# When low parts are stated, what small operations count for, and which jobs wait for which, in the front stage of a hybrid decoder layer

## The chip, the cores and the metric

The kernel runs on one core of a Trainium2 chip. The metric is the device time of one launch in microseconds (us). Engines: PE (TensorE, matmuls; PEld its weight loads), DVE (VectorE), ACT (ScalarE), POOL (GpSimd) and SP (SyncE, which issues the weight transfers).

## The reference, cut to what matters

One decoder layer for 256 tokens of width 2048, in float32:

```python
h = rms_norm(x, ln1)
proj = h @ w_in       # GDN q|k|v, beta, decay, z; MoBA q|k|v; gate A, gate B
y_a = gated_deltanet(qkv, beta, decay, z, ...) @ w_branch_a   # 8 heads, conv, delta rule
y_b = moba_attention(rope(q), rope(k), v) @ w_branch_b        # 8 heads, causal softmax
x = x + (sigmoid(gate_a) * y_a + sigmoid(gate_b) * y_b) @ w_out
h = rms_norm(x, ln2)
u = causal_dwconv(h @ w_up)
x = x + (silu(u_gate) * u_val) @ w_down
return rms_norm(x, final_norm)
```

## The kernel before

Each product of a weight block with the activations is made of three products in fp32r: the weight's high part with both parts of the activations, and its low part with the high part of the activations. A weight half tile of 128x1024 arrives by SP into `wraw`; ACT casts it to the high part `wh`, and DVE subtracts that from the raw weight, which gives the low part `wl` (`split`, L191; `load_half`, L214). There are four buffers each for `wh` and `wl`; the cast of a later half tile needs a buffer that PE has finished with.

The program is a front stage (all products with `w_in`), then the branch products, the output product, up and down. The front stage makes, for four groups of two heads, the projections for the gated delta rule (three `gdn` chunks of a convolution, one `z`), the MoBA projections (two `moba` chunks and `v` for two groups at a time), then sixteen gate chunks. Between these main matmuls it works off the small work of the heads: convolutions, the triangular solve and the delta rule (`gdn`, L633), the attention (`moba`, L867), decay and rotary.

In this stage nothing is reordered: on PE, DVE, ACT and POOL the order is that in which the program states the instructions (`manual_schedule`, L965). What sets it is an account. Each small job is a generator. `main_mm` (L177) states a main matmul, and after every 1700 units of the account, which are 16 matmuls of 128x256, it calls `tick` (L139). A tick lowers the account `load` of DVE, ACT and POOL by 1700 ns, and lets each job that is due go on to its next `yield`, if DVE's and ACT's account is under `ROOM` (quick jobs, the convolutions, have 1000 more). What a job states is added to the account by `Metered` (L84): the elements per partition times a rate plus a fixed sum per instruction. A job that yields "land" comes back `LAND` ns after its transfer.

Weight halves are stated where PE's count of main matmuls asks for them (`pump`, L156; `take`, L169): the ACT cast and, right behind it, the DVE subtraction. DVE works strictly through its own queue, so a subtraction whose cast is not over holds everything behind it.

Names used later. In `gdn`: `gam` decay factors, `jk` squared norms, `ssq` their transposes in psum, `X` and `tm` the pairs of small operations of the triangular solve (`Xa` its matrix, brought by POOL), `vb` the values that are updated step by step, `w1` (L825) the product that takes `vb`, `pot` the last transposes. In `moba`: `sc` the score products, `s_` the softmax tile with its row maxima (`largest`) and its final scaling (`share`, L911), `pT` the transposes of `s_` on PE (L932 to 934). `un`, `kq`, `vt` belong to the convolutions, `R1` is the reciprocal norm of the tokens. Psum has eight banks: three for main products, five that rotate among the small products, so that a small product in a bank waits for whoever reads the bank's former contents. Lists such as `early`, `seen`, `ended`, `clear` are gates: the job of a later group yields until the job of the former group has put itself on the list.

Of the kernel before, what the change touches and what calls it, by code (L numbers as in the profile page):

```python
# [11 lines left out]
F32 = mybir.dt.float32  # L12
# [7 lines left out]
P = 128  # L20
# [8 lines left out]
EVERY = 1700  # L29
ROOM = 2300  # L30
TABLE = 1220
ISSUE = 560
MORE = 11
LAND = 5200
TABLES = (AF.Exp, AF.Sigmoid, AF.Silu, AF.Sqrt, AF.Sin)
# [43 lines left out]
def layer_kernel(ctx: ExitStack, tc: tile.TileContext, w_first, xT, pos, cst, vec, convw, ffw, bdv,  # L79
# [4 lines left out]
    class Metered:  # L84


        def __init__(self, eng, name, per, each):
            self.eng, self.name, self.per, self.each, self.table = eng, name, per, each, None

        def __getattr__(self, op):  # L90
            f = getattr(self.eng, op)

            def run(*args, **kw):
                n = max([a.free_size() for a in (*args, *kw.values()) if hasattr(a, "free_size")], default=0)
                if op == "reciprocal":
                    n *= 6
                if op == "dma_start":
                    n = ISSUE
                func = [a for a in (*args, *kw.values()) if isinstance(a, type(AF.Exp)) and a in TABLES]
                extra = TABLE if func and func[0] != self.table else 0  # L100
                self.table = func[0] if func else self.table
                met(self.name, n * self.per + self.each, extra)
                return f(*args, **kw)  # L103

            return run

    pool = Metered(nc.gpsimd, "pool", 1.0, 0)
    act, dve = Metered(nc.scalar, "act", 0.87, 110), Metered(nc.vector, "dve", 1.03, 60)

# [14 lines left out]
    def met(name, n, more=0.0):  # L124
        load[name] += n + more
# [13 lines left out]
    def tick():  # L139
        clock[0] += EVERY  # L140
        for e in load:
            load[e] = max(load[e] - EVERY, 0.0)
        for jobs, most, soon_ in ((quick, ROOM + 1000, EVERY), (bg, ROOM, 0)):
            for it in list(jobs):
                if max(load["dve"], load["act"]) < most and ready.get(id(it), 0.0) <= clock[0] + soon_:
                    step(jobs, it)

    def flushed(jobs):
        while jobs:
            step(jobs, jobs[0])  # L150
# [18 lines left out]
    def take():  # L169
        n = taken[0]  # L170
        taken[0] += 1
        due[0] = 2 * n + 4
        passed[0] = 0
        pump()
        return n, made[2 * n:2 * n + 2]

# [14 lines left out]
    def split(hi, lo, src):  # L191
        highs.append(act.copy(hi, src))
        return low(hi, lo, src)
# [3 lines left out]

    lows, highs, again = [], [], []

# [14 lines left out]
    def load_half(raw, h, piece=HALF, at=0, into=None):  # L214
        wh, wl = halves(at, into)
        for o in range(0, HALF, piece):
            lows.append(split(wh[:, o:o + piece], wl[:, o:o + piece], raw[:, h * HALF + o:h * HALF + o + piece]))
        return wh, wl
# [355 lines left out]

    left, early, ended, joined, turned, seen, clear = [], [], [], [], [], [], []
    order_st = ExitStack()
# [46 lines left out]
    def dram(t, offset, *ap):  # L623
        return bass.AP(tensor=t.tensor, offset=t.offset + offset, ap=[list(x) for x in ap])
# [8 lines left out]
    def gdn(h0, kq, v):  # L633
# [31 lines left out]
        if left:  # L665
            turned_out()
            left.clear()
        dve.tensor_tensor(gam[:, :, 0::2, :], gam[:, :, 0:2, :], nm[:, None, None, :].to_broadcast([P, 2, 2, P]), op=ALU.add)

# [13 lines left out]
        for j in range(2):  # L683
            c = 8 + h0 + j
            for q, a in enumerate((0, 2, 1)):
                act.activation(gam[:, j, q, :], gam[:, j, q, :], AF.Exp, bias=cols[:, a, c:c + 1])
        yield
        aq0 = gl.tile([P, 2, 2, T], F32, name="aq0")
        aq1 = gl.tile([P, 2, 2, P], F32, name="aq1")
# [25 lines left out]
        pool.dma_start(dA[2:4, :P].rearrange("j s c -> s j c"), aq1[:, :, 0, :])  # L715
        while 2 * len(early) < h0:
            yield
        X = gl.tile([P, 160], F32, name="X", bufs=1)
        pool.tensor_copy(X, C["rows"])
        yield "land"  # L720
        dC = dr.tile([16, 32, 32], F32, name="dC")
        for e in range(2):
            pool.dma_start(dC[8 * e:8 * e + 8], dram(dA, e * 32 * (P + 1), (64 * (P + 1), 8), (P, 32), (1, 32)))
        yield "land"
        Xa = gl.tile([P, 33 * 32], F32, name="Xa", bufs=1)
        pool.dma_start(Xa[:, :1024], dram(dC, 0, (1024, 16), (0, 8), (1, 1024)))
        yield "land"
        pool.memset(r3(Xa, 33)[:, :, 0:1], -1.0)
# [14 lines left out]
        yield  # L743
        while 2 * len(seen) < h0:
            yield
        for q in range(4):
            pool.dma_start(S1[32 * q:32 * q + 32, :, 32 * q:32 * q + 32],
                           dram(dA, q * 64 * (P + 1) + 32, (P, 32), (2 * (P + 1) * P, 2), (1, 32)))

# [20 lines left out]
        while 2 * len(ended) < h0:  # L770
            yield
        pool.dma_start(E.rearrange("p e i c -> p (e i) c"), dram(dE, 0, (32, P), (4096, 4), (1, 32)))
        for j in range(2):
            pool.dma_start(S2[64 * j:64 * j + 64, :, 64 * j:64 * j + 64],
                           dram(dA, j * (P + 1) * P + 64, (P, 64), (2 * (P + 1) * P, 2), (1, 64)))
# [12 lines left out]
        yield  # L788
        seen.append(h0)
        Y = gl.tile([P, 2, 4, 32], F32, name="Y", bufs=1)  # L790
# [20 lines left out]
        for i in range(2):  # L811
# [10 lines left out]
            dve.tensor_tensor(vb[:, i, 1], vb[:, i, 1], pz, op=ALU.subtract)  # L822
            yield
            p1_ = sdt("w1")[:, :P]
# [4 lines left out]
            if i == 0:  # L829
                pr = r3(sdt("r1"), P)  # L830
                for j in range(2):
                    pe.matmul(pr[:, j, :], aq0[:, j, 0, P:], u[:, j, :], start=True, stop=True)
                yield
                for j in range(2):
                    for b in range(2):
                        o = slice(64 * j, 64 * j + 64)
                        dve.tensor_tensor(vb[o, 1, b], vb[o, 1, b], pr[64 * b:64 * b + 64, j, :], op=ALU.subtract)
                yield

# [16 lines left out]
        for p in range(4):  # L856
            act.mul(ot[:, p], po[:, p], st[:, 7, p:p + 1])
        yield
        pot = r3(sdt("pot"), T)
# [4 lines left out]
        yv = ya[:, h0:h0 + 2, :]  # L864
        dve.scalar_tensor_tensor(yv, pot, gnv, yv, op0=ALU.mult, op1=ALU.mult)

    def moba(h0, q, k, v):  # L867
# [58 lines left out]
        share(1)  # L926
        yield
        pps = []
# [29 lines left out]
    def delta(gr):  # L958
# [5 lines left out]
        if gr == 0:  # L964
            order_st.enter_context(tc.manual_schedule(engines={  # L965
                mybir.EngineType.DVE, mybir.EngineType.Activation, mybir.EngineType.Pool,
                mybir.EngineType.PE}))
            load.update(dve=2400.0, act=0.0, pool=0.0)
            bg.append(decay())

# [37 lines left out]
    def values_of():  # L1008
# [13 lines left out]
        v4 = m.tile([P, 2, 2 * T], F32, name="v_")  # L1022
        for i in range(2):
            act.mul(v4[:, i, :], ps[i], cols[:, 5 + i, 0:1])
        return v4
# [39 lines left out]
    for c in range(2 + MORE, 16):  # L1065
        gate(c, gts[c])
    flushed(quick)
    order_st.close()
    yp = y_st.enter_context(tc.tile_pool(name="yp", bufs=1, side="right", reuse_waits="tile"))
# [221 lines left out]
```

## Time and profile before

| what | value |
|---|---|
| median of 3 runs | 1463.87 us (1463.02 to 1464.78) |
| the profiled execution | 1462.9 us, of which the span 1461.1 us |
| mean granted TensorE clock of it | 0.996 |
| PE busy | 1439.3 us, 99% of the span |
| DVE busy | 964.5 us, 66% |
| ACT busy | 766.2 us, 52% |
| POOL busy | 186.0 us, 13% |

The span is the time from the first to the last instruction that the profiler saw. In the rows of the profile, L103 stands for every operation of ACT, DVE and POOL, because `Metered` makes them all from one line; there the names of the tiles tell which is which. A bracket at the end of a timeline row gives the idle time ahead of the instruction and what ended it.

### The profile page before, as it was taken

What the parts mean: (1) busy time and instruction counts of PE and PEld (TensorE: products, weight loads), DVE (VectorE), ACT (ScalarE), POOL (GpSimd) and SP (SyncE); (2) the same over time, 40 slices, a digit from 0 to 9 for tenths busy, and PEclk for the clock granted to TensorE, in tenths of its full rate; (3) what the DMA queues carried; (4) which work ended last, traced back from release to release, by engine and by line L of the source; (5) the groups of instructions that cost most, each with busy time, mean ns of one, the idle gap of its engine ahead of it and who ended that gap; (6) DMA issues with size and microseconds to landing.
All of it is one profiled execution on the core that took longest, in us unless ns stands there. A gap on an engine that the chain in (4) does not pass through costs nothing.

```text
span 1461.1 us, 26969 instructions
## 1 busy us (share of the span) xinstructions
PE 1439.3 (99%) x11271; PEld 1380.7 (94%) x11271; DVE 964.5 (66%) x1385; ACT 766.2 (52%) x1091; POOL 186.0 (13%) x237
## 2 busy tenths in 40 slices
PE   9999899999999999999999999999999999999998
PEld 9989898989899999999999999999999998888886
DVE  7778877786754556767776666666666666654454
ACT  7655555655564644445455545455455554444444
POOL 0003130314120300100121111111111110000000
PEclk9999999999999999999999999999999999999999
DMA  8456464646445555556685555555555555555552
GB/s 312 174 191 228 161 202 163 203 161 207 158 165 172 176 195 196 194 211 216 217 270 194 201 194 185 198 202 182 194 203 190 188 200 180 199 197 202 186 192 112
DMA packets 46347, 283.81 MB, mean 194 GB/s; under 512 B 7505, under 2 KB 8689, under 8 KB 14353
## 3 DMA queue, kind: packets, MB, share of 16 engines
q1 hardware_dynamic: 39200, 270.36, 53.4%
q0 software_dynamic: 6304, 9.63, 2.6%
q8 instruction: 88, 1.44, 0.4%
q10 hardware_dynamic: 720, 2.10, 0.4%
q14 instruction: 35, 0.28, 0.1%
HBM read 275.34 MB, written 3.82 MB: 191 GB/s over the span
## 4 chain that ended last, share of the span: by engine, by line
PE 92%; DVE 5%; ACT 2%; issue 1%; POOL 0%; DVEq 0%; ACTq 0%; POOLq 0%
PE ps_up L178 33%; PE pd L120 16%; PE ps_gate L178 11%; PE ps_gdn L178 6%; PE ps_br L178 6%; PE ps_wo L178 6%; PE ps_moba L178 5%; PE ps_v L178 3%; DVE wl L103 2%; PE ps_gdn L351 2%; PE ps_z L178 1%; ACT wh L103 1%; PE g L120 1%; DVE tm L103 0%; DVE X L103 0%
## 5 line engine op out<-in xcount | busy, mean ns | idle before, releaser
L103 DVE TENSOR_TENSOR wl<-wraw,wh 128x1024 fp32r<-128x1024 f32 (+1 forms) x496 | 611.7, 1236 | 398.4 <-ACT wh L103 395.0
L103 ACT CAST wh<-wraw 128x1024 fp32r<-128x1024 f32 (+1 forms) x496 | 515.2, 1042 | 606.0 <-PE ps_up L178 194.2
L178 PE MATMUL ps_up<-h,wh 128*128 128x256 f32 x2816 | 479.2, 276 | 0.0
L178 PEld LDWEIGHTS ps_up<-h,wh 128*128 128x128 f32 x2816 | 423.8, 188 | 0.0
L178 PE MATMUL ps_up<-h,wl 128*128 128x256 f32 x1408 | 388.8, 276 | 0.0
L178 PEld LDWEIGHTS ps_up<-h,wl 128*128 128x128 f32 x1408 | 264.3, 188 | 0.0
L178 PE MATMUL ps_gate<-hc,wh 128*128 128x256 f32 x1024 | 180.6, 280 | 0.0
L178 PEld LDWEIGHTS ps_gate<-hc,wh 128*128 128x128 f32 x1024 | 156.4, 189 | 0.0
L178 PE MATMUL ps_gate<-hc,wl 128*128 128x256 f32 x512 | 143.1, 280 | 0.0
L120 PE MATMUL pd<-wl,ah 128*128 128x512 f32 x336 | 125.4, 389 | 0.0
L120 PE MATMUL pd<-wh,al 128*128 128x512 f32 x336 | 124.4, 389 | 0.0
L120 PE MATMUL pd<-wh,ah 128*128 128x512 f32 x336 | 115.5, 389 | 0.0
L103 POOL TENSOR_TENSOR acts<-sg,cvf 128x256 f32<-128x256 f32 x44 | 62.8, 1428 | 408.1 <-ACT sg L103 396.8
L178 PE MATMUL ps_gdn<-hc,wh 128*128 128x256 f32 x640 | 111.9, 279 | 0.0
L178 PEld LDWEIGHTS ps_gdn<-hc,wh 128*128 128x128 f32 x640 | 97.2, 188 | 0.5 <-issue 0.4
L178 PEld LDWEIGHTS ps_gate<-hc,wl 128*128 128x128 f32 x512 | 97.0, 190 | 0.0
L178 PE MATMUL ps_moba<-hc,wh 128*128 128x256 f32 x512 | 90.3, 279 | 0.0
L178 PE MATMUL ps_gdn<-hc,wl 128*128 128x256 f32 x320 | 89.2, 279 | 0.5 <-DVE wl L103 0.5
L178 PE MATMUL ps_wo<-mc,wh 128*128 128x256 f32 x512 | 87.1, 276 | 0.0
L178 PEld LDWEIGHTS ps_moba<-hc,wh 128*128 128x128 f32 x512 | 78.0, 188 | 0.3 <-issue 0.2
L178 PEld LDWEIGHTS ps_wo<-mc,wh 128*128 128x128 f32 x512 | 77.0, 188 | 0.0
L120 PEld LDWEIGHTS pd<-wh,al 128*128 128x128 f32 x336 | 63.1, 188 | 13.1
(409 smaller groups left out, 1977.2 us busy)
## 6 DMA issues: line engine op xcount, KB each, us to landing
wraw<-in_w_up SPq DMA_DIRECT2D x88, 1024.0 KB, 4.9
wraw<-in_w_dn SPq DMA_DIRECT2D x44, 1024.0 KB, 4.9
wraw<-in_w_gate SPq DMA_DIRECT2D x32, 1024.0 KB, 4.9
wraw<-in_w_gdn SPq DMA_DIRECT2D x28, 1024.0 KB, 5.2
wraw<-in_w_moba SPq DMA_DIRECT2D x16, 1024.0 KB, 4.8
wraw<-in_w_o SPq DMA_DIRECT2D x16, 1024.0 KB, 4.9
wraw<-in_w_mv SPq DMA_DIRECT2D x8, 1024.0 KB, 4.9
wraw<-in_w_ba SPq DMA_DIRECT2D x8, 1024.0 KB, 4.9
```

The lines of the kernel that those rows point to most:

```text
L103: return f(*args, **kw)
L120: pe.matmul(ps, a, b, start=(start and i == 0), stop=(stop and i == n - 1), **kw)
L178: mark[0] = pe.matmul(ps, a, b, start=start, stop=stop, skip_group_check=True).ins
L351: pe.matmul(ps_two[b // 2][:, b % 2], wv[t][:, k - a, b * P:(b + 1) * P], hc.one(k, x_), start=(k == t == x_ == b % 2 == 0), stop=(k == KD ...
```

## The change

Four things are edited, all for the front stage.

1. In the front stage the DVE subtraction is no longer stated with its cast. It goes on a list `behind`, with the time at which ACT is through with the cast by the account. A tick states those whose time has come, ahead of the jobs; `take` states what is left of older tiles, in any case, before PE uses them.
2. DVE operations count at least 200 ns in the account. `ROOM` goes from 2300 to 3300, `LAND` from 5200 to 4700, `MORE` (gate chunks ahead of the end of the jobs) from 11 to 12.
3. Some gates move: `early` is waited for before `Xa` is fetched and not before `dC`; `seen` goes, and the transfers into `S1` go beside those into `S2`; a new gate `whole` stands ahead of `aq0`. The scaling of `v_` becomes a quick job, which waits for the column factors (`known`).
4. Two yields between `share` and the `pT` transposes in place of one, two ahead of `pot`.

```diff
-ROOM = 2300
+ROOM = 3300
-MORE = 11
-LAND = 5200
+MORE = 12
+WAIT = 2
+W1 = 1
+LAND = 4700
...
-                met(self.name, n * self.per + self.each, extra)
+                met(self.name, max(n * self.per + self.each, self.least), extra)
...
-    act, dve = Metered(nc.scalar, "act", 0.87, 110), Metered(nc.vector, "dve", 1.03, 60)
+    act, dve = Metered(nc.scalar, "act", 0.87, 110), Metered(nc.vector, "dve", 1.03, 60, 200)
...
             load[e] = max(load[e] - EVERY, 0.0)
+        while behind and behind[0][0] <= clock[0]:
+            behind.pop(0)[1]()
...
         pump()
+        while len(behind) > max(len(made) - 2 * n - 2, 0):
+            behind.pop(0)[1]()
...
-            lows.append(split(wh[:, o:o + piece], wl[:, o:o + piece], raw[:, h * HALF + o:h * HALF + o + piece]))
+            hi, lo, src = wh[:, o:o + piece], wl[:, o:o + piece], raw[:, h * HALF + o:h * HALF + o + piece]
+            if not stated:
+                lows.append(split(hi, lo, src))
+                continue
+            highs.append(act.copy(hi, src))
+            behind.append((clock[0] + load["act"], lambda hi=hi, lo=lo, src=src: lows.append(low(hi, lo, src))))
...
+        while 2 * len(whole) < h0 - 2:
+            yield
         aq0 = gl.tile([P, 2, 2, T], F32, name="aq0")
...
-        while 2 * len(early) < h0:
-            yield
-        X = gl.tile([P, 160], F32, name="X", bufs=1)
-        pool.tensor_copy(X, C["rows"])
         yield "land"
         dC = dr.tile([16, 32, 32], F32, name="dC")
...
+        while 2 * len(early) < h0:
+            yield
         Xa = gl.tile([P, 33 * 32], F32, name="Xa", bufs=1)
         pool.dma_start(Xa[:, :1024], dram(dC, 0, (1024, 16), (0, 8), (1, 1024)))
+        X = gl.tile([P, 160], F32, name="X", bufs=1)
+        pool.tensor_copy(X, C["rows"])
...
-        while 2 * len(seen) < h0:
-            yield
-        for q in range(4):
-            pool.dma_start(S1[32 * q:32 * q + 32, :, 32 * q:32 * q + 32],
-                           dram(dA, q * 64 * (P + 1) + 32, (P, 32), (2 * (P + 1) * P, 2), (1, 32)))
...
             dve.tensor_tensor(vb[:, i, 1], vb[:, i, 1], pz, op=ALU.subtract)
-            yield
+            yield from wait(W1)
...
         for p in range(4):
             act.mul(ot[:, p], po[:, p], st[:, 7, p:p + 1])
-        yield
+        yield from wait(2)
         pot = r3(sdt("pot"), T)
...
         share(1)
-        yield
+        yield from wait(WAIT)
         pps = []
...
             load.update(dve=2400.0, act=0.0, pool=0.0)
+            stated.append(True)
...
-        for i in range(2):
-            act.mul(v4[:, i, :], ps[i], cols[:, 5 + i, 0:1])
+
+        def scale():
+            while not known:
+                yield
+            for i in range(2):
+                act.mul(v4[:, i, :], ps[i], cols[:, 5 + i, 0:1])
+
+        quick.append(scale())
...
     flushed(quick)
+    while behind:
+        behind.pop(0)[1]()
+    stated.clear()
```

Three places show how the order on the engines moves. Numbers behind a name are those of the tile in that program, and differ between the two programs.

The first place is the start of the front stage on DVE. `R1` is the reciprocal norm of the tokens, `un` the first normed tile of a convolution, each `wl` a low part in the order in which PE uses them. Before:

```order
L103 TENSOR_TENSOR wl_455<-wraw_452,wh_454 128x1024
L103 TENSOR_TENSOR wl_459<-wraw_452,wh_458 128x1024
L103 RECIPROCAL R1_415<-R1_415 128x256
L103 TENSOR_TENSOR wl_465<-wraw_462,wh_464 128x1024
L103 TENSOR_TENSOR wl_469<-wraw_462,wh_468 128x1024
L103 TENSOR_TENSOR wl_500<-wraw_497,wh_499 128x1024
L103 TENSOR_TENSOR un_526<-ps_gdn_109,R1_415 128x512
```

After:

```order
L105 TENSOR_TENSOR wl_455<-wraw_452,wh_454 128x1024
L105 TENSOR_TENSOR sq1_0_111<-sq1_0_111,sq1_3_114 128x1024
L105 TENSOR_TENSOR wl_458<-wraw_452,wh_457 128x1024
L105 TENSOR_TENSOR sq1_0_111<-sq1_0_111 128x512
L105 TENSOR_TENSOR sq1_0_111<-sq1_0_111 128x256
L105 RECIPROCAL R1_415<-R1_415 128x256
L105 TENSOR_TENSOR un_486<-ps_gdn_109,R1_415 128x512
L105 TENSOR_TENSOR wl_463<-wraw_460,wh_462 128x1024
```

The sums of squares `sq1` now stand among the low parts, and `un` stands ahead of the third low part and no longer behind the fifth. On PE the matmul of `R1` moves from ahead of the first use of `wl_455` to 38 main matmuls later, among the uses of `wl_458`.

The same place on ACT, from the third cast on. Before:

```order
L103 CAST wh_464<-wraw_462 128x1024
L103 CAST wh_468<-wraw_462 128x1024
L103 ACT_TABLE_LOAD
L103 ACTIVATE R1_415<-R1_413,epst_65 128x256
L103 COPY z0_418<-ps_bd_396 16x256
L103 CAST wh_499<-wraw_497 128x1024
```

After:

```order
L105 CAST wh_462<-wraw_460 128x1024
L105 CAST wh_465<-wraw_460 128x1024
L105 CAST wh_499<-wraw_497 128x1024
L105 ACT_TABLE_LOAD
L105 ACTIVATE R1_415<-R1_413,epst_65 128x256
L105 COPY z0_418<-ps_bd_396 16x256
```

The cast of the fifth half tile moves from behind to ahead of the table load and `R1`.

The second place is on PE where the second group's `gdn` job begins its norms. `ssq_1981` is a transpose, `sc_1973` and `sc_1976` the score products of the first group's attention; in the program before the transposes `pT` stand in the neighbourhood and the score products far ahead. Before:

```order
L178 MATMUL ps_moba_2021<-hc_76,wl_1949 128x256
L178 MATMUL ps_moba_2021<-hc_76,wh_1948 128x256 x2
L178 MATMUL ps_moba_2021<-hc_76,wl_1949 128x256
L664 MATMUL ssq_2118<-ct_388,sqq_1946 128x128
L178 MATMUL ps_moba_2021<-hc_76,wh_1983 128x256 x2
```

After:

```order
L184 MATMUL ps_moba_1801<-hc_76,wl_1803 128x256
L903 MATMUL sc_1973<-qk1_997,qk0_871 128x256
L904 MATMUL sc_1973<-qk1_997,qk0_871 128x128
L903 MATMUL sc_1976<-qk1_997,qk0_871 128x256
L904 MATMUL sc_1976<-qk1_997,qk0_871 128x128
L675 MATMUL ssq_1981<-ct_388,sqq_1833 128x128
L184 MATMUL ps_moba_1988<-hc_76,wh_1846 128x256 x2
```

The transpose now follows the score products directly. It takes the psum bank of `sc_1973`, whose reader on DVE is `s__2018`; that is stated one tick later, behind `gam`, `jk`, `qk0`, a low part and three pairs `tm` and `X`.

The third place is on DVE, the final scaling of the second group's softmax tiles. Before, the tile is `s__2557`:

```order
L103 TENSOR_SCALAR s__2528<-s__2528,mx_2529 128x128
L103 TENSOR_TENSOR wl_2724<-wraw_2721,wh_2723 128x1024
L103 TENSOR_TENSOR tm_2738<-X_2304,Xa_2587 128x4x2
L103 TENSOR_REDUCE X_2304<-tm_2738 128x2x2
L103 TENSOR_TENSOR tm_2741<-X_2304,Xa_2587 128x4x3
L103 TENSOR_REDUCE X_2304<-tm_2741 128x2x2
L103 RECIPROCAL mx_2558<-mx_2558 128x2
L103 TENSOR_SCALAR s__2557<-s__2557,mx_2558 128x256
L103 TENSOR_SCALAR s__2557<-s__2557,mx_2558 128x128
```

After, the tile is `s__2599`:

```order
L105 TENSOR_TENSOR ya_425<-ps_z_2654,R1_415 128x512
L105 RECIPROCAL mx_2600<-mx_2600 128x2
L105 TENSOR_SCALAR s__2599<-s__2599,mx_2600 128x256
L105 TENSOR_SCALAR s__2599<-s__2599,mx_2600 128x128
L105 TENSOR_TENSOR wl_2821<-wraw_2773,wh_2820 128x1024
L105 TENSOR_TENSOR kql_2874<-kq_2158,kqh_2873 128x1024
L105 TENSOR_TENSOR wl_2858<-wraw_2855,wh_2857 128x1024
```

Before, the transposes `pT` of this tile were stated 16 main matmuls after the scaling, and a low part and two pairs `tm` and `X` stood between the two tiles' scalings; now 80 main matmuls lie between scaling and transposes, and the low parts follow behind it.

More of the change, by code (lines that the diff above doesn't have):

```diff
@@ L84, in layer_kernel, with __init__ @@
     class Metered:
-        def __init__(self, eng, name, per, each):
-            self.eng, self.name, self.per, self.each, self.table = eng, name, per, each, None
+        def __init__(self, eng, name, per, each, least=0):
+            self.eng, self.name, self.per, self.each, self.least, self.table = eng, name, per, each, least, None
         def __getattr__(self, op):
@@ L196, in three @@
         return [(ah, bh), (ah, bl), (al, bh)]
-    lows, highs, again = [], [], []
+    lows, highs, again, stated, behind = [], [], [], [], []
     HALF = 1024
@@ L573, in turned_out @@
         dve.tensor_scalar(cols[:, 0:2, :].rearrange("p a b -> p (a b)"), pt[:, :32], -1.0, None, op0=ALU.mult)
-    left, early, ended, joined, turned, seen, clear = [], [], [], [], [], [], []
+    left, early, ended, joined, turned, known, clear, whole = [], [], [], [], [], [], [], []
     order_st = ExitStack()
@@ L667, in gdn @@
             left.clear()
+            known.append(True)
         dve.tensor_tensor(gam[:, :, 0::2, :], gam[:, :, 0:2, :], nm[:, None, None, :].to_broadcast([P, 2, 2, P]), op=ALU.add)
@@ L772, in gdn @@
         pool.dma_start(E.rearrange("p e i c -> p (e i) c"), dram(dE, 0, (32, P), (4096, 4), (1, 32)))
+        for q in range(4):
+            pool.dma_start(S1[32 * q:32 * q + 32, :, 32 * q:32 * q + 32],
+                           dram(dA, q * 64 * (P + 1) + 32, (P, 32), (2 * (P + 1) * P, 2), (1, 32)))
         for j in range(2):
@@ L788, in gdn @@
         yield
-        seen.append(h0)
         Y = gl.tile([P, 2, 4, 32], F32, name="Y", bufs=1)
@@ L837, in gdn @@
                         dve.tensor_tensor(vb[o, 1, b], vb[o, 1, b], pr[64 * b:64 * b + 64, j, :], op=ALU.subtract)
-                yield
+                yield from wait(W1)
         ended.append(h0)
@@ L865, in gdn @@
         dve.scalar_tensor_tensor(yv, pot, gnv, yv, op0=ALU.mult, op1=ALU.mult)
+        whole.append(h0)
     def moba(h0, q, k, v):
@@ L926, in moba @@
         share(1)
-        yield
+        yield from wait(WAIT)
         pps = []
```

## The prediction

> **What bounds the kernel now.** I read the engine totals by stretch first. Columns: the stretch, its length, then busy time of PE, PEld, DVE, ACT and POOL, the granted TensorE clock, DMA share and GB/s.
>
> ```profile
> 40.00:470.00 430.00, 416.48 (x3340) 402.10 (x3340) 314.34 (x619) 249.29 (x420) 83.24 (x148) 0.99 0.55 182
> ```
>
> TensorE is the bound. In the stretch that the change rewrites it idles 430.00 − 416.48 = 13.5 us (the later stages keep their order, and I give them no part in the sum). Second, the waits of PE name those 13.5 us:
>
> ```profile
> PE w L825 <- DVE vb L103: 5.4, 3, 3.3
> PE pT L932 <- DVE s__2557 L103: 2.0, 1, 2.0
> PE pT L932 <- DVE s__1922 L103: 1.8, 1, 1.8
> PE pT L932 <- DVE s__1863 L103: 1.8, 1, 1.8
> PE warm L338 <- POOL ones L103: 1.0, 1, 1.0
> PE pT L932 <- DVE s__2528 L103: 0.9, 1, 0.9
> PE ps_moba L178 <- DVE wl L103: 0.8, 2, 0.5
> PE ps_gdn L178 <- DVE wl L103: 0.5, 1, 0.5
> ```
>
> Without the start's `warm` this is 13.2 us, all on DVE: 5.4 on `vb`, 6.5 on the softmax tiles `s_` ahead of the transposes `pT`, 1.3 on low parts. Third, the clock just behind those waits:
>
> ```profile
> 168.00:170.00 2.00, 2.00 (x8) 1.62 (x8) 1.86 (x3) 0.48 (x1) 0.00 (x0) 0.62 0.89 229
> 170.00:172.00 2.00, 2.00 (x9) 1.81 (x8) 0.41 (x4) 0.00 (x0) 0.00 (x0) 0.53 0.70 295
> 226.00:228.00 2.00, 2.00 (x13) 2.00 (x14) 1.83 (x8) 0.00 (x0) 0.00 (x0) 0.63 0.38 152
> 228.00:230.00 2.00, 2.00 (x11) 2.00 (x11) 1.93 (x5) 0.00 (x0) 0.00 (x0) 0.52 0.00 0
> 313.00:316.00 3.00, 3.00 (x15) 2.46 (x14) 2.96 (x5) 2.40 (x5) 2.99 (x6) 1.00 0.35 57
> 386.00:388.00 2.00, 1.47 (x9) 1.44 (x9) 1.93 (x7) 0.00 (x0) 0.00 (x0) 0.73 1.02 397
> 388.00:390.00 2.00, 2.00 (x12) 2.00 (x11) 0.68 (x3) 0.17 (x1) 0.74 (x2) 0.50 0.37 74
> ```
>
> Behind both pairs of `pT` waits and behind the 3.3 us wait on `vb`, PE runs four microseconds at half to three quarters of its clock. A stretch at clock c loses (1 − c) of its length: (0.38 + 0.47) × 2 = 1.70, (0.37 + 0.48) × 2 = 1.70, (0.27 + 0.50) × 2 = 1.54, in all 4.9 us, 1.6 for each place. Behind a smaller `vb` wait (313 to 316) it stays at 1.00. So the most that better order can give is 13.2 + 4.9 = 18.1 us.
>
> Fourth, what DVE did at such a place (start, length, last bracket the idle time before and its releaser):
>
> ```profile
> 221.40 1.23 DVE L103 TENSOR_TENSOR wl<-wraw,wh 128x1024 fp32r<-128x1024 f32 x1 [1.96 <-ACT wh L103]
> ...
> 225.21 0.55 DVE L103 TENSOR_SCALAR s__2557<-s__2557,mx 128x256 f32<-128x256 f32 x2
> ```
>
> DVE stood 1.96 us at the head of its queue with a low part whose cast was not over, with the ready softmax pieces behind it; PE waited for `s__2557` meanwhile. That is the pattern the edit goes at.
>
> **The change part by part.** Durations are those of the profiled execution: 1462.9 us, span 1461.1; the median of the runs shown is 1463.87, 1.0 above, so I sum against 1462.9 and carry the difference over to the median. The account's tick is 16 main matmuls, 1.83 us by the row of 94 below (10.72 / 94 = 0.114 each).
>
> *`pT` waits, 6.5 us and the clock of two places (3.4): gone.* After the change the last `share` is stated three ticks or more ahead of its `pT` (5.5 us), where it was one, and low parts whose cast is still out no longer stand in between. To come back, DVE would have to be 5.5 us behind.
>
> *`vb` waits, 5.4 and 1.5 of clock: gone, with the least certainty.* `w` is still stated one tick behind `vb`. What delayed `vb` were reductions of the solve and two low parts in front. The account put a small one at some 70 to 130 ns by its formula; the trace, grouped by operation (count, then busy time and mean ns of one, then the idle time before them):
>
> ```profile
> L103 DVE TENSOR_TENSOR wl<-wraw,wh 128x1024 fp32r<-128x1024 f32 x133 | 162.0, 1221 | 95.1 <-ACT wh L103 94.6
> ...
> L103 DVE TENSOR_TENSOR tm<-X,Xa 128x8 f32<-128x8 f32 (+14 forms) x60 | 13.3, 221 | 1.3
> L103 DVE TENSOR_REDUCE X<-tm 128x4 f32<-128x8 f32 (+14 forms) x60 | 11.5, 192 | 2.1
> ```
>
> With 200 ns at least, the 221 and 192 ns of a pair are counted about as they are, and `vb` has few of them in front. The wider ROOM lets 1.0 us more into the queue; ends 0 and 5.4 saved, I take 5.4.
>
> *Low-part waits, 1.3: stay.* Deferral moves a low part later, never earlier; most still have 24 to 74 matmuls (2.7 to 8.4 us) to their first use.
>
> *Fewer gates, LAND, MORE, the scaling of v as a job: nothing.* The psum bank that the scaling frees is needed over 60 main matmuls (7 us) later, the moved S1 transfers go beside S2's on POOL's queue, and an earlier solve only shifts DVE work within the stage (PE busy 416 of its 430 us, DVE 314). With LAND 0.5 us shorter, POOL stands longer at `Xa` if the transfer is not there, and SP is not involved; cover gone, this is 0.5 for each of four heads, 2 us.
>
> *New wait S, at the start.* The account of the first ticks changes, and `R1`'s matmul moves on PE from the second pair of this stage to 38 matmuls later; ACT gets a fifth cast ahead of the table load and `R1`, DVE gets RECIPROCAL and `un` ahead of `wl_463`. The rows of before:
>
> ```profile
> 30.90 0.44 PE ps_gdn L178 x2
> 31.34 0.43 PE R L394 x2
> 31.77 10.72 PE ps_gdn L178 x94
> ```
> ```profile
> 29.35 1.28 ACT L103 ACT_TABLE_LOAD   x1
> 31.81 0.47 ACT L103 ACTIVATE R<-R,epst 128x256 f32<-128x256 f32 x1 [1.18 <-PE R L394]
> 32.18 0.34 ACT L103 COPY z<-ps_bd 16x256 f32<-16x256 f32 x1
> 34.21 1.05 ACT L103 CAST wh<-wraw 128x1024 fp32r<-128x1024 f32 x1 [1.69 <-PE ps_gdn L178]
> ```
> ```profile
> 32.32 1.75 DVE L103 RECIPROCAL R<-R 128x256 f32<-128x256 f32 x1 [0.46 <-ACT R L103]
> 33.99 3.42 DVE L103 TENSOR_TENSOR wl<-wraw,wh 128x1024 fp32r<-128x1024 f32 x3
> 37.33 0.68 DVE L103 TENSOR_TENSOR un<-ps_gdn,R 128x512 f32<-128x512 f32 x1
> ```
>
> The fifth cast needs a buffer that PE frees; it began at 34.21, now 33.8, since PE reaches the place 0.43 sooner without `R1`. Then in series: cast 1.05, table 1.28, `R1` 0.47, RECIPROCAL 1.75, `un` 0.68, `wl_463` 1.23: 33.8 + 6.46 = 40.26. PE needs `wl_463` 51 matmuls in, at 30.90 + 51 × 0.114 + 0.43 = 37.14. Stall 3.1 us (2.5 if each of the six steps overlaps the last by 0.1, as neighbouring rows do; 3.6 if each hand-over costs 0.1 instead), where before nothing stood. Behind it PE has only more of the same main matmuls, so all of it is lost; DVE's next low parts gain on PE meanwhile.
>
> *New wait A, near 150 us.* `ssq_1981` now stands on PE right behind the two score products, in the bank of the first, and must wait until DVE has read it into `s__2018`, which is stated one tick later. From the end of the main matmuls at that place PE needs its score group, 1.3 us:
>
> ```profile
> 391.13 0.43 PE sc L891 x2
> 391.56 0.22 PE sc L892 x2
> ```
>
> (0.43 + 0.22, twice). DVE has, in order: `gam` 0.68, `jk` 2 × 0.29, `qk0` 0.68 (as `un`, the same shape), a low part 1.2, three pairs 3 × 0.41, `s__2018` 0.55: 4.9 us with overlaps counted twice, 4.3 without. The durations of `gam`, `jk`, `s__`:
>
> ```profile
> L103 DVE SCALAR_TENSOR_TENSOR jk<-g,ct 128x128 f32<-128x128 f32 x16 | 4.6, 288 | 1.5 <-PE g L120 1.0
> ...
> L103 DVE TENSOR_TENSOR gam<-gam,ct 128x512 f32<-128x512 f32 x4 | 2.7, 683 | 0.0
> ```
> ```profile
> 153.19 0.55 DVE L103 TENSOR_TENSOR s__1863<-sc,ct 128x384 f32<-128x384 f32 x1
> ```
>
> Stall 4.3 − 1.3 = 3.0, all of it lost, since the next tile's main matmuls queue behind `ssq_1981` on PE; ends 1.2 (the low part already done) and 4.5 (an older backlog of one low part).
>
> *Clock behind S and A.* Neither length occurs in the trace. The nearest rows are the 3.3 us wait, which lost 1.54, and the pairs of about 2 + 2, which lost 1.70. I take 1.6 each, ends 0 and 1.7. The Trainium skill, "TensorE: Matmul & The Clock Gate", section "HAM oscillation — how this bites in real kernels", puts the bound at idle gaps over about 3.4 us; by it S and A would cost no clock and the sum would be 3.2 better. The rows agree only in part: the pair at 226, with no single wait over 2.0, dropped the clock too.
>
> *A third bank wait*, `pot_4348` behind `s__4358`, stated in one tick: at most A less a tick, 3.0 − 1.83 = 1.2; I take 0.3, ends 0 and 1.2.
>
> Sum: −13.2 + 1.3 − 4.9 + 3.1 + 3.0 + 2 × 1.6 + 0.3 = −7.2: 1455.7 by the profiled execution, **1456.7** as a median.
>
> **The rivals.** (1) *S and A are not there*: DVE is ahead, or the casts come early. Then −13.2 + 1.3 − 4.9 = −16.8: 1447.1. For it: ACT stood idle 1.18 us ahead of `R1` in the rows above, so some room is there; against it: the buffer that the fifth cast needs is freed by PE itself. (2) *S and A are there, the clock stays up*: −7.2 − 3.2 = −10.4: 1453.5. For it, 313 to 316 at 1.00; against it, the pairs. This is the case in which the skill's rule on the clock holds. (3) *The change does not do at `vb` what it says*: the 5.4 and their 1.5 stay, since the wait is still one tick: −0.3, 1463.6, no change. For it: low parts still stand in the queue, 1.2 us apiece. (4) *Slower: low parts come late.* Their place: the first use of `wl` on PE, all through the front. A low part stated one or two ticks later than before, behind whatever DVE took meanwhile, holds PE for between 0.5 (the row of `ps_gdn`) and 1.83 (a tick); at 1.0 each, the gain of 7.2 is spent at 7 and 0.2% lost at 10 of the 133 that the group counts. At 17, one in eight, it is 1456.7 + 17 = 1473.7. For it: three such waits exist already and the slack after S is short; against it: 2.7 us or more of distance nearly everywhere.
>
> **How the numbers follow.** About 0.2%, 2.9 us, is what can be told from no change. Forecast 0.40, (1) 0.17, (2) 0.13, (3) 0.14, (4) 0.16. Faster: 0.40 + 0.17 + 0.13 = 0.70, less 0.02 for the forecast's upper end; same 0.14 + 0.02 = 0.16; slower 0.16, as (4) is meant from 10 low parts upward. The forecast's own range is 1451 to 1461 (S, A and clock at their ends). The range for 8 in 10 takes in (1), (2) and (3): 1446 to 1466.
>
> **What would show it.** Right: no wait of `pT` on `s_`; `w` on `vb` under 1 us; a PE wait of 2.5 to 3.6 us on `wl` at about 37 us, and one of `ssq` on `s__2018` near 150; clock near 0.6 behind each. Wrong: many waits of main matmuls on `wl` (4), `w` on `vb` as long as before (3), neither S nor A (1), or the later stages changing their time at all.

## The result and the profile after

The changed kernel takes 1451.14 us (median of 4 runs, 1448.80 to 1455.22) against 1464.32 us for the kernel before (1463.02 to 1467.59): a ratio of 0.991, 95% interval 0.9881 to 0.9938. It is faster by 13.2 us, where 7.2 was forecast. The profiled execution is the fastest of the four, 1448.8 us with a span of 1446.6.

The stretches of the changed kernel, with the columns of the rows of before:

```profile
0.00:40.00 40.00, 35.63 (x297) 33.10 (x297) 27.95 (x40) 29.01 (x44) 1.37 (x8) 1.00 0.74 285
40.00:470.00 430.00, 427.28 (x3494) 416.03 (x3495) 324.10 (x624) 255.92 (x416) 82.34 (x148) 1.00 0.58 192
```

In 40 to 470 us PE idles 430.00 − 427.28 = 2.7 us, and not 13.5. The first 40 us now hold 4.4 us of idle time, where they held 1.0. From 470 us to the end it is 7.1 us, against 7.2. The waits of PE in the changed kernel, complete:

```profile
PE ps_gdn L184 <- DVE wl L105: 3.1, 1, 3.1
PE ssq L675 <- DVE s__2018 L105: 2.7, 1, 2.7
PE warm L349 <- POOL ones L105: 1.0, 1, 1.0
PE ps_gdn L362 <- ACT wh L105: 0.3, 1, 0.3
```

Every wait of `pT`, of `w` on `vb`, and of later main matmuls on `wl` is gone, and three stand there that the kernel before did not have: 3.1 us on a low part (S of the prediction), 2.7 us on `s__2018` (A) and a small one of 0.3 us on a cast. The series behind S, on ACT and then on DVE (start, length):

```profile
33.33 1.05 ACT L105 CAST wh<-wraw 128x1024 fp32r<-128x1024 f32 x1 [4.24 <-PE ps_gdn L184]
34.40 1.28 ACT L105 ACT_TABLE_LOAD   x1
35.69 0.48 ACT L105 ACTIVATE R<-R,epst 128x256 f32<-128x256 f32 x1
```
```profile
36.20 1.75 DVE L105 RECIPROCAL R<-R 128x256 f32<-128x256 f32 x1 [4.82 <-ACT R L105]
38.06 0.69 DVE L105 TENSOR_TENSOR un<-ps_gdn,R 128x512 f32<-128x512 f32 x1
38.66 1.22 DVE L105 TENSOR_TENSOR wl<-wraw,wh 128x1024 fp32r<-128x1024 f32 x1
```

The fifth cast waits 4.24 us for PE to free its buffer, and the table load, `R1`, RECIPROCAL, `un` and the low part follow one upon the other, until PE goes on at 39.94. The low part itself takes 1.2 us; what is late is that it stands behind RECIPROCAL, which stands behind a cast. The chain of waits shows A the same way:

```profile
161.67 1.05 ACT wh L105
...
162.75 1.23 DVE wl L105
...
165.26 0.47 DVE s__2018 L105
...
165.78 0.33 PE ssq L675
```

PE was through with its score products at 163, and waits there for a cast, its low part, three pairs of the solve and `s__2018`. The rows of ACT and DVE ahead of that:

```profile
160.27 0.68 DVE L105 TENSOR_TENSOR gam<-gam,ct 128x512 f32<-128x512 f32 x1
161.67 1.04 ACT L105 CAST wh<-wraw 128x1024 fp32r<-128x1024 f32 x1 [3.60 <-PE ps_moba L184]
162.75 1.23 DVE L105 TENSOR_TENSOR wl<-wraw,wh 128x1024 fp32r<-128x1024 f32 x1 [0.27 <-ACT wh L105]
```

`gam`, which the prediction's sum has in this series, was through before the main matmuls ended at 161.65. The cast, which that sum does not have, stands in the series. One thing is not as forecast: the clock behind both.

```profile
40.00:42.00 2.00, 2.00 (x18) 2.00 (x19) 1.93 (x4) 0.00 (x0) 0.00 (x0) 1.00 0.00 0
42.00:44.00 2.00, 2.00 (x20) 2.00 (x19) 2.00 (x3) 1.05 (x1) 0.00 (x0) 1.00 0.49 66
166.00:168.00 2.00, 2.00 (x19) 2.00 (x19) 0.54 (x3) 0.00 (x0) 0.00 (x0) 1.00 0.98 414
168.00:170.00 2.00, 2.00 (x19) 2.00 (x19) 0.07 (x1) 1.13 (x2) 0.00 (x0) 1.00 0.05 21
```

It stays at 1.00. In this execution S and A cost their idle time and no more.

### The profile page after: what moved, and what is told of

It is laid out like the page before. It is cut to its first block, busy times and chain, and to the rows that moved or that the text cites. A ratio compares the mean times of both kernels' runs of the same rounds, so it can differ in the third digit from the quotient of the medians.

```text
span 1446.6 us, 26965 instructions
## 1 busy us (share of the span) xinstructions
PE 1432.4 (99%) x11271; PEld 1376.7 (95%) x11271; DVE 962.7 (67%) x1385; ACT 768.3 (53%) x1093; POOL 185.1 (13%) x237
## 4 chain that ended last, share of the span: by engine, by line
PE 98%; DMA 1%; ACT 1%; DVE 0%; SPq 0%; issue 0%; DVEq 0%; ACTq 0%
PE ps_up L184 33%; PE pd L122 17%; PE ps_gate L184 12%; PE ps_gdn L184 7%; PE ps_moba L184 6%; PE ps_br L184 6%; PE ps_wo L184 6%; PE ps_v L184 3%; PE ps_z L184 3%; PE ps_gdn L362 1%; PE g L122 1%; DMA first<-in_first 1%; PE po L122 0%; PE py_b L957 0%; ACT wh L105 0%; PE sc L903 0%
## 5 line engine op out<-in xcount | busy, mean ns | idle before, releaser
L122 PEld LDWEIGHTS pd<-wl,ah 128*128 128x128 f32 x336 | 63.1, 188 | 13.2
```

Source lines behind the costliest of these rows:

```text
L122: pe.matmul(ps, a, b, start=(start and i == 0), stop=(stop and i == n - 1), **kw)
```

## The experiments

Each is timed against the kernel before on the same chip. The median of the kernel before lay between 1463.67 and 1464.35 us in the three series, so a difference between runs of two series can be off by some 0.7. Ratios carry 95% intervals. The theory: three of the edits (deferral, the account, the spacing) each clear DVE's queue at the `pT` and `vb` waits, and the deferral alone brings S and A. Rivals stand in the expectations.

### The two new waits taken away

```diff
-            if not stated:
+            if not stated or len(made) < 4:
```

> Edit: the low parts of the first four half tiles are stated right behind their casts again; all else as in the changed kernel. With that R1's matmul is back ahead of wl_455, un stands behind the low parts again, and in the order that follows ssq of the second group no longer stands behind the score products. Theory (the two new waits S and A cost 3.1 and 2.7 us and nothing hides them): no PE wait on wl near 37 us, none of ssq on s__; 1448.8 - 5.8 = 1443.0 by the profile, give or take 1.2 for a new bank wait of sc on ya; median 5 to 6 us under the changed kernel's. Rival (the waits only take up slack that is then lost elsewhere, since DVE is behind by as much): other PE waits of 3 us or more in all, median within 2 us of the changed kernel's 1451.

Measured: 1444.41 us (1443.71 to 1444.90), ratio 0.9867 (0.9852 to 0.9882). The waits of PE:

```profile
PE warm L349 <- POOL ones L105: 1.0, 1, 1.0
PE sc L903 <- DVE ya L105: 1.0, 1, 1.0
```

Both waits are gone, and the bank wait of `sc` is the one that was expected with up to 1.2. The profiled execution went from 1448.8 to 1444.9 us: 5.8 less for S and A, 0.3 less for the small wait on a cast, 1.0 more for `sc`, and 1.2 more that lies in PE's busy time (1433.6 against 1432.4) and is not explained. S and A are real losses of the change, and they can be had back by stating four low parts earlier. (A goes because the order further on comes out differently; the edit does not touch the place.) The scatter shrinks with them: 1.2 us here against 6.4 in the changed kernel.

### Without the deferral

```diff
-            if not stated:
+            if True:
```

> Edit: low parts are stated with their casts throughout, as before; account, gates and waits as in the changed kernel. Theory (deferral, the account and the spacing each remove waits, S and A come from the deferral): S and A gone (-5.8), but the head of DVE's queue is held by low parts again, so waits on wl (1.3) and on vb (2 to 5) come back: 1448 to 1452 by the profile. Rival 1 (deferral is worth nothing once spacing and account are there): 1443 to 1444. Rival 2 (deferral is the main thing): pT and vb waits of 8 us or more, 1456 or more.

Measured: 1445.70 us (1445.29 to 1446.48), ratio 0.9875 (0.9859 to 0.9892). The waits of PE:

```profile
PE w L836 <- DVE vb L105: 1.4, 1, 1.4
PE warm L349 <- POOL ones L105: 1.0, 1, 1.0
PE w L824 <- DVE vb L105: 0.7, 1, 0.7
PE pu L807 <- DVE Y L105: 0.3, 1, 0.3
```

The kernel without the deferral is faster than the changed one by 5.4 us. A little comes back on `vb` (2.1 us, as expected), nothing on `wl` and nothing on `pT`. So the deferral as it is written costs more than it brings once the other edits are there. Rival 2 is out; rival 1 is nearly right, and the theory's 1448 to 1452 was missed (1446.5 by the profile).

DVE's own waits fit that. First the changed kernel, then the one without deferral, from 40 to 470 us:

```profile
DVE wl L105 <- ACT wh L105: 85.6, 67, 4.1
```
```profile
DVE wl L105 <- ACT wh L105: 86.2, 72, 3.5
```

DVE stands at the head of its queue with a low part whose cast is not over for as long with the deferral as without it. With PE's waits in this run at 2.4 us in all, `warm` left out, those 86 us are mostly harmless; only those count behind which something stands that PE needs.

### One yield to pT

```diff
-WAIT = 2
+WAIT = 1
```

> Edit: one yield between the last share and the pT transposes, as before; all else as in the changed kernel. Theory (pT waits went because of deferral and account as much as of spacing): S and A stay, one or two pT waits of up to 2 us at groups where one tick lies between: 1449 to 1453 by the profile. Rival (the spacing alone removed them): pT waits of 4 to 6.5 us and the clock loss of 1.7 behind each pair: 1455 to 1459.

Measured: 1452.31 us (1450.92 to 1452.78), ratio 0.992 (0.9905 to 0.9934), no different from the changed kernel. The first two waits of PE:

```profile
PE ps_gdn L184 <- DVE wl L105: 3.1, 1, 3.1
PE ssq L675 <- DVE s__2018 L105: 2.7, 1, 2.7
```

No wait of `pT` came back, so the rival is out: with the deferral and the account in place, the second yield is not needed. The profiled execution, 1452.8 us, has the same S and A as the changed kernel's, and is 4.0 us longer. Here is why:

```profile
40.00:42.00 2.00, 1.79 (x13) 1.79 (x14) 1.90 (x5) 0.00 (x0) 0.00 (x0) 0.92 0.00 0
42.00:44.00 2.00, 2.00 (x11) 2.00 (x11) 2.00 (x3) 0.00 (x0) 0.00 (x0) 0.50 0.42 57
44.00:46.00 2.00, 2.00 (x15) 2.00 (x15) 1.83 (x2) 1.04 (x1) 0.00 (x0) 0.73 0.71 291
168.00:170.00 2.00, 2.00 (x12) 2.00 (x11) 0.48 (x3) 0.00 (x0) 0.00 (x0) 0.50 0.97 410
170.00:172.00 2.00, 2.00 (x14) 2.00 (x14) 0.00 (x0) 0.00 (x0) 0.00 (x0) 0.66 0.01 4
```

In this execution both waits cost clock as well: (0.08 + 0.50 + 0.27) × 2 = 1.70 us behind S and (0.50 + 0.34) × 2 = 1.68 behind A, together 3.4 of the 4.0. The edit can't be the reason: it acts between the last scaling and the first `pT` (193.9 us in the changed kernel), later than both places.

### Without the 200 ns

```diff
-    act, dve = Metered(nc.scalar, "act", 0.87, 110), Metered(nc.vector, "dve", 1.03, 60, 200)
+    act, dve = Metered(nc.scalar, "act", 0.87, 110), Metered(nc.vector, "dve", 1.03, 60, 0)
```

> Edit: small DVE operations count by the formula alone again (least 0); all else as in the changed kernel. Theory (counting them at 200 ns is what keeps the solve from standing in front of vb): S stays, A goes with the other order (-2.7), PE waits on vb of 3 to 5 us come back, one long enough to cost 1.5 of clock: 1448 to 1453 by the profile. Rival (deferral alone cleared the way for vb): no wait on vb over 0.5, 1446.

Measured: 1448.16 us (1446.69 to 1450.01), ratio 0.9894 (0.9879 to 0.9908). S stays with 3.1 us, A is gone, as expected; no wait on `vb` came back, which the theory wanted, so the rival holds here: with deferral and the wider ROOM the count of the small operations is not needed. Against the first experiment, which has neither S nor A, S is worth about 3.75 us in the medians (the two kernels differ in the count of 200 ns as well).

### The spacing alone

On the kernel before:

```diff
-        yield
+        yield from wait(2)
         pps = []
```

> Edit: the kernel before, with two yields in place of one between the last share and pT; nothing else. Theory (each of deferral, account and spacing clears pT by itself): the pT waits of 6.5 us go and the clock of the two places (3.4) with them; the waits on vb (5.4, and 1.5 of clock) and on wl (1.3) stay: 1462.9 - 9.9 = 1453.0 by the profile, median about 1454. Rival (the DVE backlog behind the pT waits moves on and is paid at the next wait): 1458 or more.

Measured: 1461.51 us (1458.95 to 1462.73, 10 runs), ratio 0.9979 (0.997 to 0.9989). The largest wait of PE:

```profile
PE w L825 <- DVE vb L103: 8.6, 4, 3.3
```

The rival holds. The `pT` waits are gone, and 8.6 − 5.4 = 3.2 us of them stand one product further, at a wait of `w` on `vb` that ends near 225 us and that the kernel before did not show (5.4 in three there, 8.6 in four here). The transposes had been hiding it: `vb` stood behind the same DVE work as `s__2557`. The drop of the clock stayed there as well (0.73, 0.50 and 0.92 from 224 us on). At the other pair of `pT` waits, near 166 us, 0.9 (`g` on `kql`) and 0.7 (`ssq` on the copy of `pT`) came in place of 3.6, and the drop is gone. So most of a stall that was removed without shortening the work in front of it was paid at a later consumer; the median gained 2.2 us.

### Neither deferral nor spacing

```diff
-            if not stated:
+            if True:
...
-WAIT = 2
+WAIT = 1
```

> Edit: the changed kernel with low parts stated with their casts, and with one yield between share and pT; what stays is the account (200 ns, ROOM 3300), the gates, LAND, MORE, pot and the job for v. Theory (account and gates keep DVE's backlog short enough for one tick): pT waits of at most 2 us in all at two of four groups, vb about 2 as in the run without deferral: 1445 to 1449 by the profile. Rival (without deferral the spacing is what carries pT): pT waits of 4 us or more with a clock loss, 1451 to 1456.

Measured: 1447.68 us (1447.21 to 1448.11), ratio 0.9883 (0.9869 to 0.9897). The waits are word for word those of the kernel without deferral and with two yields (1.4 and 0.7 on `vb`, 0.3 on `Y`), and the ratios' intervals overlap. No `pT` wait, though only one yield stands between scaling and transposes again: the account and the gates are enough.

### The gates alone

The run above, with the account of before:

```diff
-ROOM = 3300
+ROOM = 2300
...
-    act, dve = Metered(nc.scalar, "act", 0.87, 110), Metered(nc.vector, "dve", 1.03, 60, 200)
+    act, dve = Metered(nc.scalar, "act", 0.87, 110), Metered(nc.vector, "dve", 1.03, 60, 0)
```

> Edit: the changed kernel without deferral, with least 0, ROOM 2300 and one yield to pT; what stays is the moved gates, LAND 4700, MORE 12, two yields ahead of pot and the job for v. Theory (the gates gave nothing): the waits of the kernel before come back nearly whole, pT 4 to 6.5 and vb 3 to 5.4 us, with clock: 1457 to 1463 by the profile. Rival (moving early, seen and whole spreads the solve and is what cleared vb): pT waits stay, vb waits under 1 us, 1453 to 1456.

Measured: 1460.92 us (1458.18 to 1461.83, 10 runs), ratio 0.9974 (0.9964 to 0.9984). The largest waits of PE:

```profile
PE pT L944 <- DVE s__1842 L105: 2.0, 1, 2.0
PE pT L944 <- DVE s__2555 L105: 2.0, 1, 2.0
PE pT L944 <- DVE s__1918 L105: 1.8, 1, 1.8
PE w L836 <- DVE vb L105: 1.3, 1, 1.3
```

The `pT` waits are all back. The `vb` waits are not: 1.8 us in all (1.3 and 0.5) against 5.6 (5.4 and 0.2). So the moved gates, or what goes with them in this run (LAND, MORE, `pot`, the job for v), are what thinned out `vb`; theory and rival each have half. From here to the run above it is 13.2 us, for the 200 ns and ROOM alone.

### Which of the three clears pT

Each of these adds to the gates alone one of the three; with ROOM comes the second yield as well. The 200 ns:

```diff
-    act, dve = Metered(nc.scalar, "act", 0.87, 110), Metered(nc.vector, "dve", 1.03, 60, 0)
+    act, dve = Metered(nc.scalar, "act", 0.87, 110), Metered(nc.vector, "dve", 1.03, 60, 200)
```

> Edit: the run with the gates alone (1460.9 median, PE waits on pT 7.3 and vb 1.8 us) plus the 200 ns for small DVE operations; no deferral, ROOM 2300, one yield to pT. Theory (the count of the small operations is what clears DVE's queue): pT waits under 1 us, vb 2 us, a bank wait of sc of up to 1.2: 1446 to 1450 median. Rival (the wider ROOM did it, since jobs then run earlier): pT waits of 4 us or more with their clock loss, 1455 or more.

ROOM, with two yields to `pT`:

```diff
-ROOM = 2300
+ROOM = 3300
...
-WAIT = 1
+WAIT = 2
```

> Edit: the run with the gates alone plus ROOM 3300 and two yields to pT; no deferral, least 0. Theory (the count is what clears the queue): a wider ROOM lets more in, so waits on vb of 3 us or more stay, with clock: 1452 to 1460 median. Rival (ROOM did it): no wait over 1.5 us, 1445 to 1449.

The deferral, save the first four half tiles:

```diff
-            if True:
+            if not stated or len(made) < 4:
```

> Edit: the run with the gates alone plus the deferral of low parts, save the first four half tiles; least 0, ROOM 2300, one yield to pT. Theory (a low part at the head of DVE's queue is the larger part of each pT wait): pT waits 2 us or less in all, vb 1 to 2, no clock loss: 1446 to 1451 median. Rival (deferral is worth nothing without the account): pT 5 to 7 us with clock, 1457 or more.

| added to the gates alone | median us | range | ratio (95% interval) | PE waits on `pT`, on `vb` |
|---|---|---|---|---|
| nothing | 1460.92 | 1458.18 to 1461.83 | 0.9974 (0.9964 to 0.9984) | 7.3, 1.8 |
| 200 ns | 1448.42 | 1447.82 to 1448.77 | 0.9891 (0.9877 to 0.9904) | 0.2, 0 |
| ROOM 3300, two yields | 1449.16 | 1448.51 to 1449.50 | 0.9896 (0.9882 to 0.9909) | 1.2, 2.3 |
| deferral | 1446.05 | 1445.78 to 1446.59 | 0.9876 (0.9861 to 0.9891) | 0, 0 |

With the deferral alone, apart from `warm`, one wait is left:

```profile
PE sc L903 <- DMA qk<-Xc: 0.5, 1, 0.5
```

Each of the three runs is some 12 to 15 us faster than the gates alone; all three additions, with S and A cured, make 16.5 together (1460.92 to 1444.41). They are three ways to the same gain, not three gains. (All stand on the moved gates; none was tried with the old ones. ROOM without the second yield was not tried either, so what ROOM does by itself is not shown.) For ROOM the expectation failed: a wider ROOM was to let more into DVE's queue (1452 to 1460), and 1449.2 is close to what the rival gave (1445 to 1449). Why it helps is not settled; that jobs get through earlier, and the long queue of the solve falls elsewhere, was not measured apart.

### Both cures and more room at w1

```diff
-            if not stated:
+            if not stated or len(made) < 4:
...
-W1 = 1
+W1 = 2
```

> Edit: as in the first experiment (low parts of the first four half tiles stated at once), and two yields in place of one between vb and w1. Theory (what is left there is one wait of sc of 1.0 us, whose bank neighbour this order no longer has): no PE wait over 0.5 us apart from the start, 1444.9 - 1.0 to 1.2 = 1443.7 by the profile, median 1443 to 1444. Rival (the later delta rule pushes the last jobs behind the gates and PE runs dry there): 1446 or more.

Measured: 1443.36 us (1443.12 to 1443.94), ratio 0.9854 (0.984 to 0.9868), the fastest kernel here, 7.8 us under the changed one. The waits of PE:

```profile
PE warm L349 <- POOL ones L105: 1.0, 1, 1.0
PE sc L903 <- ACT ot L105: 0.5, 1, 0.5
```

From 40 to 470 us PE idles 430.00 − 429.45 = 0.55 us: there is next to nothing left to win from order.

### A longer first wait

```diff
             un = un_ if now else begin()
+            if not joined:
+                for _ in range(1):
+                    nc.vector.tensor_tensor(un, ps, R1b, op=ALU.mult)
             joined.append(ps)
```

> Edit: the changed kernel with the first un made twice on DVE (the same values, not in the account), which lengthens the wait S from 3.1 to about 3.75 us; the order is the same. Theory on the clock (a single idle time of 2.9 to 3.3 us costs 1.7 us of clock in some executions and not in others, a longer one in every one): S 3.7 to 3.8, clock near 0.5 behind it for 3 to 4 us, 1451 to 1453 by the profile and 0.65 + up to 1.7 over the changed kernel's median of 1451.1. Rival (the clock has nothing to do with the length of the wait): 0.65 more and the same scatter as the changed kernel.

Measured: 1454.39 us (1453.38 to 1454.95, 5 runs), ratio 0.9931 (0.9919 to 0.9943); the profiled execution 1454.1. The waits and the clock behind them:

```profile
PE ps_gdn L184 <- DVE wl L105: 3.8, 1, 3.8
PE ssq L678 <- DVE s__2019 L105: 2.7, 1, 2.7
```
```profile
38.00:40.00 2.00, 0.00 (x0) 0.00 (x0) 1.97 (x3) 0.56 (x2) 0.00 (x0) 0.93 0.02 4
40.00:42.00 2.00, 1.41 (x6) 1.41 (x7) 1.90 (x5) 0.35 (x1) 0.00 (x0) 0.50 0.00 0
42.00:44.00 2.00, 2.00 (x12) 2.00 (x11) 2.00 (x2) 0.00 (x0) 0.00 (x0) 0.50 0.00 0
44.00:46.00 2.00, 2.00 (x11) 2.00 (x11) 1.29 (x2) 0.48 (x1) 0.00 (x0) 0.50 0.93 262
46.00:48.00 2.00, 2.00 (x17) 2.00 (x16) 1.40 (x2) 0.57 (x1) 0.00 (x0) 0.86 0.98 414
168.00:170.00 2.00, 0.79 (x5) 0.79 (x6) 1.84 (x7) 0.00 (x0) 0.00 (x0) 0.86 0.80 205
170.00:172.00 2.00, 2.00 (x11) 2.00 (x11) 0.00 (x1) 0.00 (x0) 0.00 (x0) 0.50 0.76 320
172.00:174.00 2.00, 2.00 (x16) 2.00 (x15) 0.00 (x0) 0.18 (x1) 0.00 (x0) 0.79 0.00 0
```

0.65 us more of waiting made the median 3.25 us longer, and the scatter fell from 6.4 to 1.6. Behind S the clock was at half for nearly seven microseconds. Counting only time in which PE was busy, that lost 0.50 × (1.41 + 2 + 2) + 0.14 × 2 = 3.0 us, where the theory had 1.7. Behind A it fell as well: 0.14 × 0.79 + (0.50 + 0.21) × 2 = 1.5 us. With the longer wait (0.7) that makes 5.2 of the 5.3 us by which this execution is longer than the profiled one of the changed kernel; the theory's 1451 to 1453 was missed by the part of A and the longer drop. That the clock drops behind so long a wait in every execution is not shown: there is one profile of it. The times of the five runs fit it: 0.7 more, with a drop behind A and none behind S, would make 1451.0 of 1448.8, and the shortest run took 1453.38.

## Why the prediction was right, and where it was off

*The bound: right in what it is made of, some 2 us too low.* It was 13.2 us of waits and 4.9 of clock, 18.1. The kernel with both cures, which has neither, is 1462.9 − 1443.25 = 19.6 us faster by the profiled executions (20.5 by its median against the forecast's 1463.87). The bound left out 0.2 of clock (0.91 from 390 to 392 us, behind the rows of 386 to 390) and a wait of 0.2 on `vb`, and a gap costs more than its row says, as worked out below.

*`pT` gone: right, for a reason that was half wrong.* The prediction gave the three ticks of spacing as the reason, and the low parts. With one yield nothing came back (third and sixth experiments), and the spacing alone moved much of the stall to `vb` (fifth). On the moved gates the 200 ns alone clear it but for 0.2 us, the deferral alone does wholly, and ROOM with the second yield leaves 1.2.

*`vb` gone: right, for a reason that was mostly wrong.* It was put down to the 200 ns. The gates with LAND, MORE, `pot` and the job for v, held to give nothing, took 5.6 to 1.8. The 200 ns take the rest, but so does the deferral without them.

*Low-part waits of 1.3 stay: wrong.* They went. The deferral alone is enough for that, and so is ROOM with the second yield; with the 200 ns alone 0.9 of them is there still.

*S: right in place, cause and size; A: right in its bank and its reader, and in size partly by luck.* For S 3.1 was forecast and 3.1 measured, by the series that was forecast. This is what reading the order against the durations of before can do: the wait does not occur in the trace of before. For A 3.0 was forecast and 2.7 measured, at 163 us and not near 150. The sum for A had `gam`, `jk` and `qk0` (1.9 us) between the end of the main matmuls and the low part. `gam` and `jk` were over by then, `qk0` ran beside a cast, and what held the low part up (1.1 us) was this cast, which ACT could not start until PE had freed its buffer. *The third bank wait*, 0.3: not there.

*Clock behind S and A, 1.6 each: the term that was mis-sized.* It was 0 in the profiled execution and 3.4 in the third experiment's, behind the same two waits and the same instructions up to there, so it is a matter of the execution. The changed kernel's times spread over 6.4 us, from 1448.80 upward, while kernels without long waits spread over 0.8 to 1.2; the median lies 2.3 above the profiled execution, somewhere between no loss and both. The slowest, 1455.22, is further up than 3.4 explains. Its mean granted clock was 0.995 where the other three had 0.998; it has no trace, and where it lost the rest is open.

The sum, then, by the profiled execution, 1462.9 to 1448.8: −13.2 − 4.9 + 3.1 + 2.7 = −12.3 of −14.1. The rest is 1.8, or 2.1 with the new 0.3 on the cast. Of that, 0.4 are the clock and the `vb` wait that the bound left out. Most of what is left is probably that a gap costs more than its row in the waits: a main matmul that is followed by another takes 0.114 us, while the last one ahead of a gap shows 0.28 us busy. By an estimate from these two that is 0.17 us for each of eleven waits before and three after, so 1.4. Against the forecast of −7.2 the 6.9 of difference are 3.2 of clock, 1.3 of low parts, 0.3 and 0.3 at A and the bank, and that 1.8.

*The rivals.* (2), the clock stays up, is what the profiled execution did: 1453.5 less the low parts and the rest. (1) did not occur, but the first experiment builds it: 1444.41 against the 1447.1 that was worked out. (3) is out, and (4) as well: no main matmul waited for a low part except at S.

The rule of the Trainium skill ("TensorE: Matmul & The Clock Gate", section "HAM oscillation — how this bites in real kernels") that idle gaps must be over about 3.4 us gave the profiled execution right and the third experiment's wrong: behind waits of 2.7 and 3.1 us the clock fell to 0.50 there. The same page of the Trainium skill, section "The HAM clock gate (the "warmup" mystery)", says that the window in which PE's activity is watched is free-running. So where a wait falls in it can differ between executions, which would fit the scatter. It would not by itself explain a drop behind a wait that is shorter than the window, and no run here tried it.

## What to carry to other kernels

When an edit states work later, walk the first use of each late piece on the bound engine, above all at the start, where there is no backlog to hide behind, and look at which instruction now owns the psum bank that the next small product takes. Test the parts of a combined edit singly: here three of them (ROOM with a second yield) each bought the same 12 to 15 us, and one, the deferral, brought 5.8 us of new waits. And where the clock behaves as in these traces, a wait of 2.7 to 3.3 us should be priced as itself plus a chance of 1.7; the one of 3.8 us cost itself and 3.0.

## What the runs showed of the hardware

The granted clock behind one and the same wait differs between executions. Behind the 3.1 us at S it stayed at 1.00 in the changed kernel and in the run without the 200 ns, and went to 0.92, 0.50 and 0.73 in the third experiment. Behind the 2.7 us at A it stayed at 1.00 in the changed kernel, and went to 0.50 and 0.66 in the third experiment and to 0.86, 0.50 and 0.79 in the last. Behind waits on `vb` of 3.1 to 3.3 us it fell in all three that were traced (one in the kernel before, two with the spacing alone). Each of these drops lost 1.5 to 1.7 us.

Behind 3.8 us it began to fall while PE was still idle (0.93 from 38 to 40 us, PE busy 0.00) and stayed at 0.50 for three windows of 2 us, a loss of 3.0 us. If it went straight to 0.50, it fell at about 39.7 us, some 2.9 us after PE had gone idle at 36.8; this is an estimate from the window's 0.93 and from the 0.78 us that PE was busy between 36 and 38 us.
